# Thirteen instead of twelve seven-product blocks per MLP layer, another order of their loads, and tiles moved into the pool

## The chip, the cores and the metric

The kernel runs on one core of a Trainium2 chip. The metric is the device time of one execution in microseconds. A core has several engines with an instruction queue each: TensorE (PE, matrix products), VectorE (DVE), ScalarE (ACT), GpSimd (POOL) and SyncE (SP, which here only starts transfers), and 16 DMA engines that all queues share.

## The reference

A trunk of two layers over 256 tokens of width 2048, in float32. Each layer adds a mixer and then an MLP:

```python
x = x + mixer(rms_norm(x, norm_mix[l]))
h = rms_norm(x, norm_ffn[l])
u = jnp.einsum('bsd,df->bsf', h, w_up[l])             # 2048 -> 8192
x = x + jnp.einsum('bsf,fd->bsd', jnp.square(jax.nn.relu(u)), w_down[l])   # 8192 -> 2048
```

Layer 0's mixer is a sliding-window attention beside a state-space scan, layer 1's a dilated attention. The change lies in the MLPs' second product, the down projection; what it does in the mixers is to hold a few tiles elsewhere.

## The kernel before

**Three-product matmuls.** Every weight comes from HBM as float32 and is split into a rounded part `whi` and a rest `wlo`; the activations likewise. A product is three matmuls: hi*hi, hi*lo, lo*hi. Weights come in pieces of 256 rows by 512 columns (512 KB, two k-tiles). A plain piece works on both halves of the tokens: 2 k-tiles x 2 halves x 3 = 12 matmuls of 128x512.

**The MLP.** An up unit is 512 hidden columns: 8 pieces, 16 units per layer. Its squared ReLU is transposed into `uf` and split into `uh` and `ul`. Two up units make a chunk of 1024 hidden columns, c = 0 to 7. The down projection takes, for each chunk, four column stripes of 512, four pieces each.

**Seven.** For a chunk c and a pair of stripes, the down product can be seen as 2x2 blocks (two token halves; two halves of the chunk; two stripes), which the class `Seven` does with seven block products instead of eight. With its two halves h of each product it is 14 pieces of 6 matmuls, 84 in all, where the same work in plain units is 8 pieces of 12, 96 in all. The weight blocks are called 11, 21, 12, 22 (first digit the half of the chunk, second the stripe), each with two halves (a, b below). A seven loads 8 of them on SP's queue (`sraw`, line 262). Block sums are made in place: GpSimd starts a transfer that adds the neighbouring stripe's block to 11 and to 12 in SBUF (accumulating DMA, line 276; written 11' and 12' below), and DVE adds twice two tiles (t2 = 11' + 22, and 21 += t2). The products come in the order of the tuple SEVEN: P1 (11), P2 (21), Q6 (t2), Q7 (12'), Q5 (11'), Q4 (21'), Q3 (22). On the side of the activations P1, P2 and Q4 use halves of u, the other four use sums s1 and s2 that `operands(c)` makes. P1 is the only one that uses the first u tile of the chunk, and only its first 128 tokens. Before, 12 of the 14 pairs of chunks 0 to 6 in a layer are sevens: both pairs in chunks 0, 1, 3, 4 and 5, one in chunks 2 and 6. Chunk 7 is plain.

**The order of work.** `mlp` writes a plan, a list of pieces, which `mixed` interleaves: after the first 16 up pieces, each chunk gets n up pieces from the tuple (20, 20, 8, 20, 20, 24, 0), and the sevens' pieces are put between them from 4.5 up pieces on. So each chunk starts with five pure up pieces, then comes the first seven's first piece (P1, half a). The plan is carried out by `run`, piece by piece. At piece i it issues, in this order: `low(i+2)` (DVE: wlo = raw - whi; for a seven's P1 and P2 the accumulating transfer is issued right behind it, since it changes a raw tile whose parts have just been taken), `fetch(i+6)` (SP: the transfer of the raw tile; for a seven at P1 it fetches 11, at P2 it fetches 21, 12 and 22), `high(i+3)` (ACT: whi), `add(i+4)` (DVE sums), evictions, and the matmuls. Up pieces' raw tiles turn in a ring of RAW = 4 buffers (`wraw`, line 306), so an up piece's transfer waits on SP's queue until DVE has made the `wlo` of the up piece four before, and what stands behind it on SP's queue waits with it. The sevens' raw tiles come from the common pool `work`, tag `w4`, of 29 tiles of 4 KB per partition. The engines' side work (transposes, splits, sums, norms) is put between by `tick`, which keeps a budget per piece. All engines run their instructions in the order of emission; line 71 is the helper through which DVE, ACT and PE instructions pass.

Of the kernel before, what the change touches and what calls it, by code (L numbers as in the profile page):

```python
# [7 lines left out]
F32 = mybir.dt.float32  # L8
# [32 lines left out]
def trunk(ctx: ExitStack, tc: tile.TileContext, x, norm_mix, norm_ffn, w_up, w_down, ab_w_in, ab_q_norm,  # L41
# [193 lines left out]
    def unit(*a, **k):  # L235
# [1 line left out]

    SEVEN = (("P1", "a", "11"), ("P2", "b", "21"), ("Q6", "a", "t2"), ("Q7", "c", "12"), ("Q5", "a", "11"),  # L240
             ("Q4", "c", "21"), ("Q3", "a", "22"))
    LOADS = {"P1": ("11",), "P2": ("21", "12", "22")}
    SUMS = {"Q6": ("t2", "11", "22"), "Q4": ("21", "21", "t2")}

    class Seven:


        def __init__(self, w, rows, c0, kts, operands, to, needs, mark):
            self.w, self.rows, self.c0, self.operands, self.to, self.needs, self.mark = \
                w, rows, c0, operands, to, needs, mark  # L250
# [8 lines left out]
        def fetch(self, p, h):  # L259
            for b in LOADS.get(SEVEN[p][0], ()):  # L260
                r, c = self.rows[int(b[0]) - 1] + h * KC, self.c0 + (int(b[1]) - 1) * W
                nc.sync.dma_start(self.tile(b, h),
                                  self.w[r * 128:(r + KC) * 128, c:c + W].rearrange("(k p) c -> p k c", p=128))

        def add(self, p, h):
            if SEVEN[p][0] in SUMS:
# [1 line left out]
                x, y = self.raw[x, h], self.raw[y, h]  # L268
                V.tensor_tensor(self.raw[o, h] if o != "t2" else self.tile(o, h), x, y, op=OP.add)

        def accumulate(self, p, h):

            o = {"P1": ("11", 0), "P2": ("12", 1)}.get(SEVEN[p][0])
            if o is not None:
                r, c = self.rows[o[1]] + h * KC, self.c0 + W
                nc.gpsimd.dma_start(self.raw[o[0], h],  # L276
                                    self.w[r * 128:(r + KC) * 128, c:c + W].rearrange("(k p) c -> p k c", p=128),
                                    accum_op=OP.add)

        def source(self, p, h):  # L280
            return self.raw[SEVEN[p][2], h]
# [1 line left out]
        def evict(self, p):  # L283

            name, b, _ = SEVEN[p]
            t, j, op = {"P1": (0, 0, OP.add), "P2": (0, 0, OP.add), "Q6": (1, 0, OP.add), "Q7": (1, 1, OP.subtract),
                        "Q5": (1, 1, OP.subtract), "Q4": (1, 0, OP.add), "Q3": (0, 1, OP.subtract)}[name]
            r = self.to[t][j]
            V.tensor_tensor(r, r, self.bank[b], op=op)

    def run():
        todo = plan
# [31 lines left out]
        def low(i):  # L324
            if i < len(todo):
                raw = raws.pop(i)
                lo = wpool.tile([128, KC, raw.shape[2]], F32R, name="wlo", bufs=AHEAD + 1)
                V.tensor_tensor(lo, raw, f32(parts[i][0]), op=OP.subtract)
                parts[i].append(lo)
                u, c = todo[i]  # L330
                if isinstance(u, Seven):
                    u.accumulate(*c)

        for i in range(RAW):
            if i % 2 == 0:
# [8 lines left out]
                load_x(2 + i // 2)  # L344
            fetch(RAW + i)
        high(AHEAD)
        nc.sync.dma_start(cst[:, C_TRI:], shapes[:, C_TRI:])
        pending = []
        before = ps = None
        kept, held = [], []  # L350
        for i, (u, c) in enumerate(todo):
# [9 lines left out]
            if isinstance(u, Seven):  # L361
                p, h = c
                name, b, _ = SEVEN[p]
                if p in u.needs and h == 0:
                    need(u.needs[p])
                new = b not in u.bank
                if new:
                    u.bank[b] = aux("sp")
                sp = u.bank[b]
                xh, xl, t0 = u.operands(name)  # L370
# [250 lines left out]
                last(t, j)  # L621
        free(ps)

    def residual_unit(w, ktiles, j, needs={}, nm=None, last=None, check=None, mark=None):
        def after(ps):
            if check is not None:
                check()
# [323 lines left out]
    def mlp(layer, nm, nxt, last=None):  # L951
# [22 lines left out]
        def operands(c):  # L974

            for k in marks[c - 1] if 0 < c < NC - 2 else [("up", layer)] if c else []:
                yield from until(k)
            if c == NC - 1:
                yield from until(("uf", layer, 2 * c + 1))
            for i in (2 * c, 2 * c + 1):  # L980
                yield from until(("uf", layer, i))
                u[i] = slot("uh"), slot("ul")
                split(u[i][0], u[i][1], uf[i])
                done.add(("u", layer, i))
                yield 2
            if c == NC - 1:
                return
            a1, a2 = uf[2 * c], uf[2 * c + 1]
            s1, s2 = w4([128, 4, T], "s1"), w4([128, 4, T], "s2")
            o, n = slice(0, 128), slice(128, T)  # L990
            V.tensor_tensor(s1[:, :, o], a2[:, :, n], a1[:, :, n], op=OP.subtract)
            V.scalar_tensor_tensor(s1[:, :, n], a1[:, :, o], -1.0, s1[:, :, o], op0=OP.mult, op1=OP.subtract)
            V.tensor_tensor(s2[:, :, o], a1[:, :, o], a1[:, :, n], op=OP.subtract)
            V.scalar_tensor_tensor(s2[:, :, n], a2[:, :, o], -1.0, s1[:, :, n], op0=OP.mult, op1=OP.subtract)
            yield 2
            sums[c] = [(slot("sh"), slot("sl")) for _ in range(2)]
            for (h, l), s in zip(sums[c], (s1, s2)):
                split(h, l, s)
                yield 1
# [12 lines left out]
        def down(c, j):  # L1012
# [6 lines left out]
            def whole():  # L1019
                assert all(("down", layer, k, j) in done or ("down", layer, k, j - j % 2) in done for k in range(NC - 1))  # L1020

            return residual_unit(wd, kts, j, {4 * b: ("u", layer, 2 * c + b) for b in range(2)}, nxt, last, whole).pieces

        def seven(c, j):
            def parts(name):
                i, k, t = {"P1": (0, 0, 0), "P2": (0, 1, 0), "Q4": (0, 1, 128), "Q5": (1, 0, 0), "Q6": (1, 0, 128),
                           "Q7": (1, 1, 0), "Q3": (1, 1, 128)}[name]
                return (sums[c][k] if i else u[2 * c + k]) + (t,)

            marks[c].append(("down", layer, c, j))  # L1030
            return Seven(wd, (8 * c, 8 * c + 4), j * W, 4, parts,
                         [[res[:, t, (j + i) * W:(j + i + 1) * W] for i in range(2)] for t in range(2)],
                         {0: ("u", layer, 2 * c), 1: ("u", layer, 2 * c + 1), 2: ("sums", layer, c)},
                         marks[c][-1]).pieces

        def mixed(rest, s, start, end):

# [20 lines left out]

    n2 = Norm(R_MIX + 16, False)
    mlp(0, n1, n2)  # L1060
# [2 lines left out]
    wqkv = c_w_qkv[0]  # L1063
    oh, ol = [None] * 4, [None] * 4

    def dilated(g):
# [105 lines left out]
```

## Time and profile before

| | |
|---|---|
| time, median of 3 | 2264.33 us (2263.88 to 2264.35) |
| profiled execution, its own time | 2264.74 us |
| its span, first to last instruction | 2262.9 us |
| granted TensorE clock, mean | 1.000 |
| DMA moved | 475.10 MB, 210 GB/s in the mean |
| SP-issued `sraw` loads | 192 of 512 KB, median 8.1 us to landing |
| POOL-issued accumulating `sraw` transfers | 96 of 512 KB, median 10.7 us to landing |
| `wraw` loads of w_up | 256 of 512 KB, median 5.2 us to landing |

The profile records one execution: when each instruction ran on its engine, what released it, and when each transfer landed. Groups of instructions are written as out<-in with the program's tile names; a time to landing is counted from the issue on the queue. Matmuls overlap: one is shown as 389 ns while the next starts before it ends, so the time per matmul is read from a long row of them.

### The profile page before, as it was taken

The page shows a single profiled execution, that of the slowest core. Times are in us where ns is not written, and L with a number is a line of the kernel's source. Part 1 is how long each engine was busy: PE and PEld are TensorE (multiplying, and loading weights), DVE is VectorE, ACT ScalarE, POOL GpSimd, SP SyncE. Part 2 cuts the span into 40 slices and gives each one's busy share as a digit, 9 for nine tenths or more (in the row PEclk, how much of TensorE's full clock was granted, in tenths as well). Part 3 has the DMA queues.
Part 4 walks back from the last instruction along what each step waited for, and adds up shares of the span by engine and source line. Part 5 has one row for each costly group of instructions (what it writes and reads, how often), then busy time and mean ns, then how long its engine had stood idle before and what let it go on. Part 6 is the DMA issues. An engine that isn't in the chain of part 4 may idle for free.

```text
span 2262.9 us, 30235 instructions
## 1 busy us (share of the span) xinstructions
PE 2247.2 (99%) x11029; PEld 1873.0 (83%) x11029; DVE 1749.7 (77%) x2482; ACT 1290.0 (57%) x1615; POOL 125.7 (6%) x116
## 2 busy tenths in 40 slices
PE   8999999999999999999999999999999999999999
PEld 7998988888888888888788778778888888888877
DVE  6779986556888888887976766665588888888786
ACT  6565545445666556565664555555566665656663
POOL 1000000000001010000000000000000000010000
PEclk9999999999999999999999999999999999999999
DMA  7546555568797797888756455546788789797874
GB/s 235 163 142 190 177 177 182 190 186 246 216 296 214 209 288 222 242 245 234 219 171 192 149 158 168 168 151 186 245 237 240 206 242 281 207 282 228 248 222 141
DMA packets 255318, 475.10 MB, mean 210 GB/s; under 512 B 17156, under 2 KB 27696, under 8 KB 255168
## 3 DMA queue, kind: packets, MB, share of 16 engines
q1 hardware_dynamic: 218976, 416.34, 56.7%
q0 software_dynamic: 26624, 50.48, 12.5%
q10 hardware_dynamic: 9568, 6.34, 0.9%
q8 instruction: 86, 1.41, 0.2%
q14 instruction: 64, 0.52, 0.1%
HBM read 470.97 MB, written 2.13 MB: 209 GB/s over the span
## 4 chain that ended last, share of the span: by engine, by line
PE 97%; DMA 1%; DVE 1%; issue 1%; ACT 0%; SPq 0%; DVEq 0%; POOLq 0%; ACTq 0%
PE acc L71 71%; PE sp L71 20%; PE uT L71 1%; PE sc L71 1%; PE o L71 1%; DMA sraw<-in_w_down_dram 1%; PE pT L71 1%; PE yp L71 1%; PE xT L71 1%; DVE wlo L71 1%; DMA wraw<-in_ab_w_in_dram 0%; PE qp L71 0%; DMA res<-in_x_dram 0%; PE yo L71 0%; PE kp L71 0%
## 5 line engine op out<-in xcount | busy, mean ns | idle before, releaser
L71 ACT ACTIVATE whi<-wraw 128x1024 fp32r<-128x1024 f32 (+1 forms) x600 | 631.9, 1054 | 493.6 <-PE acc L71 350.8
L71 DVE TENSOR_TENSOR wlo<-wraw,whi 128x1024 fp32r<-128x1024 f32 (+1 forms) x600 | 725.0, 1214 | 233.7 <-PE acc L71 159.7
L71 PE MATMUL acc<-whi,hThi 128*128 128x512 f32 (+1 forms) x1632 | 647.7, 397 | 1.8 <-ACT hThi L71 1.7
L71 PE MATMUL acc<-whi,hTlo 128*128 128x512 f32 (+1 forms) x1632 | 634.8, 389 | 1.0 <-DVE hTlo L71 1.0
L71 PE MATMUL acc<-wlo,hThi 128*128 128x512 f32 (+1 forms) x1632 | 634.1, 389 | 0.7 <-DVE wlo L71 0.7
L71 ACT ACTIVATE whi<-sraw 128x1024 fp32r<-128x1024 f32 x336 | 353.7, 1059 | 292.4 <-DVE sraw L71 137.0
L71 DVE TENSOR_TENSOR wlo<-sraw,whi 128x1024 fp32r<-128x1024 f32 x336 | 408.8, 1221 | 85.3 <-PE acc L71 35.3
L71 PEld LDWEIGHTS acc<-whi,hThi 128*128 128x128 f32 x1632 | 307.6, 188 | 66.8 <-issue 5.8
L71 PEld LDWEIGHTS acc<-whi,hTlo 128*128 128x128 f32 x1632 | 307.2, 188 | 65.7 <-DVE hTlo L71 1.8
L71 PEld LDWEIGHTS acc<-wlo,hThi 128*128 128x128 f32 x1632 | 307.9, 189 | 60.9 <-DVE wlo L71 1.1
L276 POOL DMA_DIRECT2D sraw<-in_w_down_dram x96 | 117.3, 1576 | 2058.7 <-DVE wlo L71 1815.6
L71 PE MATMUL sp<-wlo,sh 128*128 128x512 f32 x384 | 149.5, 389 | 0.0
L71 PE MATMUL sp<-whi,sl 128*128 128x512 f32 x384 | 149.5, 389 | 0.0
L71 PE MATMUL sp<-whi,sh 128*128 128x512 f32 x384 | 149.4, 389 | 0.0
L71 DVE TENSOR_TENSOR sraw<-sraw 128x1024 f32<-128x1024 f32 x96 | 117.1, 1219 | 26.4 <-DMA sraw<-in_w_down_dram 26.3
L71 DVE TENSOR_TENSOR res<-res,sp 128x512 f32<-128x512 f32 x168 | 114.7, 682 | 17.4 <-PE sp L71 17.1
L71 PE MATMUL acc<-hThi,whi 128*128 128x256 f32 x384 | 112.3, 293 | 0.0
L71 PE MATMUL sp<-whi,ul 128*128 128x512 f32 x288 | 112.1, 389 | 0.0
L71 PE MATMUL sp<-whi,uh 128*128 128x512 f32 x288 | 112.0, 389 | 0.0
L71 PE MATMUL sp<-wlo,uh 128*128 128x512 f32 x288 | 112.0, 389 | 0.0
L71 PE MATMUL acc<-hThi,wlo 128*128 128x256 f32 x384 | 108.5, 283 | 0.0
L71 PE MATMUL acc<-hTlo,whi 128*128 128x256 f32 x384 | 108.5, 283 | 0.0
(221 smaller groups left out, 2749.8 us busy)
## 6 DMA issues: line engine op xcount, KB each, us to landing
wraw<-in_w_up_dram SPq DMA_DIRECT2D x256, 512.0 KB, 5.2
sraw<-in_w_down_dram SPq DMA_DIRECT2D x192, 512.0 KB, 8.1
wraw<-in_ab_w_in_dram SPq DMA_DIRECT2D x96, 512.0 KB, 3.7
sraw<-in_w_down_dram POOLq DMA_DIRECT2D x96, 512.0 KB, 10.7
wraw<-in_c_w_qkv_dram SPq DMA_DIRECT2D x96, 512.0 KB, 4.2
wraw<-in_w_down_dram SPq DMA_DIRECT2D x64, 512.0 KB, 4.2
wraw<-in_ab_w_out_dram SPq DMA_DIRECT2D x48, 512.0 KB, 3.7
wraw<-in_c_w_o_dram SPq DMA_DIRECT2D x32, 512.0 KB, 3.6
```

Source lines behind the costliest of these rows:

```text
L71: return f(out, *a, **k)
L276: nc.gpsimd.dma_start(self.raw[o[0], h], self.w[r * 128:(r + KC) * 128, c:c + W].rearrange("(k p) c -> p k c", p=128), accum_op=OP.add)
```

## The change

Thirteen of the fourteen pairs per layer become sevens: chunk 2 now has both. The up pieces per chunk become 19, 18, 18, 19, 19, 19. The pool grows from 29 to 31 tiles; masks, the keys `k0T` and `btok` are no longer held for the whole kernel but as tiles of the pool, and the second transfer of constants is cut in two (128 KB and 192 KB where 704 KB went, the rest loaded in layer 1). Of a chunk's first u only the half that P1 reads is split and kept, hi and lo in one tile (chunks 0 to 5). In a seven, Q7 and Q6 change places; at P1 the blocks 12 and 11 are fetched, at P2 21 and 22; the accumulating transfer into 12 is issued by GpSimd at once behind the issue of 12's load, instead of behind P2's `low`; that into 11 stays behind P1's `low`. Chunk 7's u no longer waits for both its tiles.

```diff
-    work = ctx.enter_context(tc.tile_pool(name="work", bufs=29))
+    work = ctx.enter_context(tc.tile_pool(name="work", bufs=31))
...
-    cst = consts.tile([128, C_ALL], F32, name="cst")
+    cst = consts.tile([128, C_M0], F32, name="cst")
...
-    mask0 = cst[:, C_M0:C_M0 + 384]
-    mask1 = cst[:, C_M1:C_M1 + 384]
-    mult1 = cst[:, C_N1:C_N1 + 384]
+    mask0 = w4([128, 384], "mask0")
...
-    SEVEN = (("P1", "a", "11"), ("P2", "b", "21"), ("Q6", "a", "t2"), ("Q7", "c", "12"), ("Q5", "a", "11"),
+    SEVEN = (("P1", "a", "11"), ("P2", "b", "21"), ("Q7", "c", "12"), ("Q6", "a", "t2"), ("Q5", "a", "11"),
              ("Q4", "c", "21"), ("Q3", "a", "22"))
-    LOADS = {"P1": ("11",), "P2": ("21", "12", "22")}
+    LOADS = {"P1": ("12", "11"), "P2": ("21", "22")}
...
                 nc.sync.dma_start(self.tile(b, h),
                                   self.w[r * 128:(r + KC) * 128, c:c + W].rearrange("(k p) c -> p k c", p=128))
+                if b == "12":
+                    self.accumulate("12", 1, h)
...
-        def accumulate(self, p, h):
-
-            o = {"P1": ("11", 0), "P2": ("12", 1)}.get(SEVEN[p][0])
-            if o is not None:
-                r, c = self.rows[o[1]] + h * KC, self.c0 + W
-                nc.gpsimd.dma_start(self.raw[o[0], h],
-                                    self.w[r * 128:(r + KC) * 128, c:c + W].rearrange("(k p) c -> p k c", p=128),
-                                    accum_op=OP.add)
+        def accumulate(self, b, half, h):
+
+            r, c = self.rows[half] + h * KC, self.c0 + W
+            nc.gpsimd.dma_start(self.raw[b, h],
+                                self.w[r * 128:(r + KC) * 128, c:c + W].rearrange("(k p) c -> p k c", p=128),
+                                accum_op=OP.add)
...
                 u, c = todo[i]
-                if isinstance(u, Seven):
-                    u.accumulate(*c)
+                if isinstance(u, Seven) and c[0] == 0:
+                    u.accumulate("11", 0, c[1])
...
-        nc.sync.dma_start(cst[:, C_TRI:], shapes[:, C_TRI:])
+        nc.sync.dma_start(cst[:, C_TRI:], shapes[:, C_TRI:C_M0])
+        nc.sync.dma_start(mask0, shapes[:, C_M0:C_M1])
...
-                    wh, wl = xh[:, q, t0:t0 + 128], xl[:, q, t0:t0 + 128]
+                    wh, wl = xh[:, q, th:th + 128], xl[:, q, tl:tl + 128]
...
-    k0T = consts.tile([128, 2, T], F32, name="k0T")
+    kb = w4([128, 2, W], "kb")
+    k0T = kb[:, 0].rearrange("p (h t) -> p h t", h=2)
...
-    btok = consts.tile([128, 4, 128], F32, name="btok")
+    btok = kb[:, 1].rearrange("p (g n) -> p g n", g=4)
...
-            if c == NC - 1:
-                yield from until(("uf", layer, 2 * c + 1))
             for i in (2 * c, 2 * c + 1):
                 yield from until(("uf", layer, i))
-                u[i] = slot("uh"), slot("ul")
-                split(u[i][0], u[i][1], uf[i])
+                if i % 2 == 0 and c < NC - 2:
+                    u[i] = slot("uhl")
+                    split(u[i][:, :, :128], u[i][:, :, 128:], uf[i][:, :, :128])
+                else:
+                    u[i] = slot("uh"), slot("ul")
+                    split(u[i][0], u[i][1], uf[i])
...
-        for c, n in enumerate((20, 20, 8, 20, 20, 24, 0)):
+        for c, n in enumerate((19, 18, 18, 19, 19, 19, 0)):
             x, o = ups[o:o + n], o + n
             if c == NC - 2:
                 x = sum((down(c, j) for j in (0, 1)), []) + sum((down(c + 1, j) for j in range(NS)), [])
                 mixed(x, seven(c, 2), 2, 19)
-            elif n == 8:
-                mixed(x + down(c, 2) + down(c, 3), seven(c, 0), 4.5, 16)
             else:
-                mixed(x, seven(c, 0) + seven(c, 2), 4.5, n + (3 if n == 24 else 0))
+                mixed(x, seven(c, 0) + seven(c, 2), 4.5, n + (3 if c == NC - 3 else 0))
...
+            if g == 0 and i == 0:
+                masks.append(w4([128, 2, 384], "masks"))
+                nc.sync.dma_start(masks[0], shapes[:, C_M1:].rearrange("p (a k) -> p a k", a=2))
+            mask1, mult1 = masks[0][:, 0], masks[0][:, 1]
```

Of the last chunk's bookkeeping (`early`, `ready`, `sevens_end`) only the place is changed in which the next norm's sums and the stores are started.

SyncE's queue at the first seven of chunk 1 in layer 0, before. `wraw` are up pieces; `sraw_6009` is 11a, 6044 is 11b, 6066, 6068 and 6070 are 21a, 12a and 22a, 6121, 6123 and 6125 are 21b, 12b and 22b; `wraw_6021` is the up piece behind P1's first half, `wraw_6095` the one behind P2's first half:

```order
L306 DMA wraw_5991<-in_w_up_dram 128x2x512
L262 DMA sraw_6009<-in_w_down_dram 128x2x512
L306 DMA wraw_6021<-in_w_up_dram 128x2x512
L262 DMA sraw_6044<-in_w_down_dram 128x2x512
L262 DMA sraw_6066<-in_w_down_dram 128x2x512
L262 DMA sraw_6068<-in_w_down_dram 128x2x512
L262 DMA sraw_6070<-in_w_down_dram 128x2x512
L306 DMA wraw_6095<-in_w_up_dram 128x2x512
L262 DMA sraw_6121<-in_w_down_dram 128x2x512
L262 DMA sraw_6123<-in_w_down_dram 128x2x512
L262 DMA sraw_6125<-in_w_down_dram 128x2x512
L306 DMA wraw_6161<-in_w_up_dram 128x2x512
```

The same place after. `sraw_5991` is 12a, 5994 is 11a, 6006 is 12b, 6009 is 11b, then 6053 and 6055 are 21a and 22a, 6080 and 6082 are 21b and 22b:

```order
L306 DMA wraw_5967<-in_w_up_dram 128x2x512
L260 DMA sraw_5991<-in_w_down_dram 128x2x512
L260 DMA sraw_5994<-in_w_down_dram 128x2x512
L260 DMA sraw_6006<-in_w_down_dram 128x2x512
L260 DMA sraw_6009<-in_w_down_dram 128x2x512
L306 DMA wraw_6031<-in_w_up_dram 128x2x512
L260 DMA sraw_6053<-in_w_down_dram 128x2x512
L260 DMA sraw_6055<-in_w_down_dram 128x2x512
L260 DMA sraw_6080<-in_w_down_dram 128x2x512
L260 DMA sraw_6082<-in_w_down_dram 128x2x512
L306 DMA wraw_6109<-in_w_up_dram 128x2x512
L306 DMA wraw_6148<-in_w_up_dram 128x2x512
```

The loads of 12 have moved ahead of those of 11: 12a from the sixth entry of this stretch to the second, 12b from the tenth to the fourth. 21b stands ninth in both. The up piece behind P2's first half (`wraw_6095`, now `wraw_6109`) has moved from the eighth entry to the eleventh, behind all eight loads of the seven.

GpSimd's queue at the same place, before: the four accumulating transfers into 11a, 11b, 12a and 12b, then the first of the chunk's second seven:

```order
L276 DMA sraw_6009<-in_w_down_dram 128x2x512
L276 DMA sraw_6044<-in_w_down_dram 128x2x512
L276 DMA sraw_6068<-in_w_down_dram 128x2x512
L276 DMA sraw_6123<-in_w_down_dram 128x2x512
L276 DMA sraw_6386<-in_w_down_dram 128x2x512
```

After: 12a, 12b, 11a, 11b, then the second seven's first:

```order
L274 DMA sraw_5991<-in_w_down_dram 128x2x512
L274 DMA sraw_6006<-in_w_down_dram 128x2x512
L274 DMA sraw_5994<-in_w_down_dram 128x2x512
L274 DMA sraw_6009<-in_w_down_dram 128x2x512
L274 DMA sraw_6349<-in_w_down_dram 128x2x512
```

The two transfers into 12 now stand ahead of those into 11, and the first of them waits for nothing but the landing of its own load.

More of the change, by code (lines that the diff above doesn't have):

```diff
@@ L236, in unit, with __init__ @@
         plan.extend(Unit(*a, **k).pieces)
-    SEVEN = (("P1", "a", "11"), ("P2", "b", "21"), ("Q6", "a", "t2"), ("Q7", "c", "12"), ("Q5", "a", "11"),
+    SEVEN = (("P1", "a", "11"), ("P2", "b", "21"), ("Q7", "c", "12"), ("Q6", "a", "t2"), ("Q5", "a", "11"),
              ("Q4", "c", "21"), ("Q3", "a", "22"))
-    LOADS = {"P1": ("11",), "P2": ("21", "12", "22")}
+    LOADS = {"P1": ("12", "11"), "P2": ("21", "22")}
     SUMS = {"Q6": ("t2", "11", "22"), "Q4": ("21", "21", "t2")}
     class Seven:
-        def __init__(self, w, rows, c0, kts, operands, to, needs, mark):
-            self.w, self.rows, self.c0, self.operands, self.to, self.needs, self.mark = \
-                w, rows, c0, operands, to, needs, mark
+        def __init__(self, w, rows, c0, kts, operands, to, needs, mark, after=None):
+            self.w, self.rows, self.c0, self.operands, self.to, self.needs, self.mark, self.after = \
+                w, rows, c0, operands, to, needs, mark, after
             self.halves = kts // KC
@@ L289, in evict @@
             V.tensor_tensor(r, r, self.bank[b], op=op)
+            if p == 6 and self.after is not None:
+                self.after()
     def run():
@@ L369, in run @@
                 sp = u.bank[b]
-                xh, xl, t0 = u.operands(name)
+                xh, xl, th, tl = u.operands(name)
                 tick(True)
@@ L622, in add_stripe, with residual_unit @@
         free(ps)
-    def residual_unit(w, ktiles, j, needs={}, nm=None, last=None, check=None, mark=None):
+    def residual_unit(w, ktiles, j, needs={}, nm=None, last=None, mark=None):
         def after(ps):
-            if check is not None:
-                check()
             add_stripe(ps, j, last)
@@ L1017, in down, with after, ready, sevens_end @@
                                      mark=marks[c][-1]).pieces
-            def whole():
-                assert all(("down", layer, k, j) in done or ("down", layer, k, j - j % 2) in done for k in range(NC - 1))
-            return residual_unit(wd, kts, j, {4 * b: ("u", layer, 2 * c + b) for b in range(2)}, nxt, last, whole).pieces
+            def after(ps):
+                if early[j]:
+                    add_stripe(ps, j, last)
+                else:
+                    add_stripe(ps, j)
+                early[j] += 1
+                ready(j, False)
+            return Unit([(wd, j * W, W)], kts, after,
+                        needs={4 * b: ("u", layer, 2 * c + b) for b in range(2)}).pieces
+        early = [1, 1, 0, 0]
+        def ready(j, stored=True):
+            if early[j] == 2:
+                if last is not None and stored:
+                    for t in range(2):
+                        last(t, j)
+                if nxt is not None:
+                    nxt.begin(j)
+        def sevens_end(j):
+            for k in (j, j + 1):
+                early[k] += 1
+                ready(k)
         def seven(c, j):
@@ L1027, in parts @@
                            "Q7": (1, 1, 0), "Q3": (1, 1, 128)}[name]
-                return (sums[c][k] if i else u[2 * c + k]) + (t,)
+                if name == "P1" and c < NC - 2:
+                    return u[2 * c], u[2 * c], 0, 128
+                return (sums[c][k] if i else u[2 * c + k]) + (t, t)
             marks[c].append(("down", layer, c, j))
@@ L1033, in seven @@
                          {0: ("u", layer, 2 * c), 1: ("u", layer, 2 * c + 1), 2: ("sums", layer, c)},
-                         marks[c][-1]).pieces
+                         marks[c][-1], (lambda: sevens_end(j)) if c == NC - 2 else None).pieces
         def mixed(rest, s, start, end):
@@ L1064, in trunk @@
     oh, ol = [None] * 4, [None] * 4
+    masks = []
     def dilated(g):
```

## Prediction

> **What bounds the kernel now.** I read the page first, then the chain of waits, then what PE waits for. The page's first part, and its fourth, the chain that ended last:
>
> ```profile
> PE 2247.2 (99%) x11029; PEld 1873.0 (83%) x11029; DVE 1749.7 (77%) x2482; ACT 1290.0 (57%) x1615; POOL 125.7 (6%) x116
> ...
> PE 97%; DMA 1%; DVE 1%; issue 1%; ACT 0%; SPq 0%; DVEq 0%; POOLq 0%; ACTq 0%
> ```
>
> PE is the chain. Its waits, by what ended them (total us, times, longest):
>
> ```profile
> PE acc L71 <- ACT uh L71: 1.5, 2, 0.7
> PE acc L71 <- DVE ul L71: 1.2, 2, 0.6
> PE acc L71 <- DVE wlo L71: 1.1, 2, 0.7
> ```
>
> The MLPs lose under 4 us to waits. So the change can gain what PE no longer computes and hardly more, but it can lose as much as it makes PE wait. A PE piece costs 6 or 12 matmuls; a long row of them in the chain gives the price of one:
>
> ```profile
> 461.45 29.95 PE acc L71 x132
> ```
>
> 29.95 / 132 = 0.2269 us. A plain piece is 2.72 us, a seven's piece 1.36 us.
>
> **The gain.** Per layer one pair of stripes goes from 96 matmuls to 84: 24 fewer in all, 24 x 0.2269 = 5.45 us off the chain. The second wait for a wlo goes too, I think. It is the one row of PE's timeline in which a seven's sum came late:
>
> ```profile
> 1902.16 0.50 PE L71 MATMUL acc<-wlo,hThi 128*128 128x512 f32 x1 [0.67 <-DVE wlo L71]
> ```
>
> The chain ahead of it runs through the accumulating transfer into 11, which t2 needed; t2 is now needed two pieces later, and the transfer starts no later. With the pipeline's refill I count 0.9 us. The waits for uh and ul belong to chunk 6, whose split isn't touched, and stay.
>
> **What DVE and ACT get.** In place of 8 plain pieces come 14, with 4 sums and 7 evictions for 4:
>
> ```profile
> L71 DVE TENSOR_TENSOR wlo<-sraw,whi 128x1024 fp32r<-128x1024 f32 x336 | 408.8, 1221 | 85.3 <-PE acc L71 35.3
> L71 DVE TENSOR_TENSOR sraw<-sraw 128x1024 f32<-128x1024 f32 x96 | 117.1, 1219 | 26.4 <-DMA sraw<-in_w_down_dram 26.3
> L71 DVE TENSOR_TENSOR res<-res,sp 128x512 f32<-128x512 f32 x168 | 114.7, 682 | 17.4 <-PE sp L71 17.1
> L71 ACT ACTIVATE whi<-sraw 128x1024 fp32r<-128x1024 f32 x336 | 353.7, 1059 | 292.4 <-DVE sraw L71 137.0
> ```
>
> DVE: 6 x 1.22 + 4 x 1.22 + 3 x 0.68 = 14.3 us more per layer; the halved splits give back 6 x about 0.6 = 3.6. A chunk of 18 up pieces and two sevens keeps PE for 18 x 2.72 + 28 x 1.36 = 87 us. DVE's work in it: 46 wlo, 8 sums, 14 evictions, and some 10 us of splits and sums of u, 56 + 10 + 10 + 10 = 86 us by these durations. It is less in truth, since neighbours on DVE overlap by about 5 hundredths (two `sl` of 1.22 us took 2.35 in the timeline):
>
> ```profile
> 636.99 2.35 DVE L71 TENSOR_TENSOR sl<-s,sh 128x1024 fp32r<-128x1024 f32 x2
> ```
>
> So DVE just keeps up, and I take nothing for it; were it bound, 2 us in each of four such chunks, 8 us, would be its price. ACT has room. The masks' later load (384 KB) and the two pool tiles lie in layer 1's mixer, where a load lands in 4.2 us in the median:
>
> ```profile
> wraw<-in_c_w_qkv_dram SPq DMA_DIRECT2D x96, 512.0 KB, 4.2
> ```
>
> They are wanted far later than that: nothing, and about 1 us if that cover were gone.
>
> **The loads, where I expect the loss.** SP's and GpSimd's queues at a first seven, here that of chunk 1 in layer 0. PE starts its P1 at 641.49 (T0):
>
> ```profile
> 641.49 0.39 PE L71 MATMUL sp<-whi,uh 128*128 128x512 f32 x1
> ```
>
> ```profile
> 624.92 0.62 SPq L262 DMA_DIRECT2D sraw<-in_w_down_dram  x1
> ...
> 633.80 0.85 SPq L306 DMA_DIRECT2D wraw<-in_w_up_dram  x1
> ```
>
> ```profile
> 637.37 1.20 POOL L276 DMA_DIRECT2D sraw<-in_w_down_dram  x1 [47.37 <-DVE wlo L71]
> 641.92 3.68 POOL L276 DMA_DIRECT2D sraw<-in_w_down_dram  x3 [3.34 <-DVE wlo L71]
> ```
>
> SP issues the first block 16.6 us ahead of T0, the accumulating transfers come 4.1 us ahead of it and later, when nearly all of the seven's loads have landed. That lead is set by SP's wait for the ring of four `wraw` buffers, which the change leaves alone:
>
> ```profile
> SPq L306 <- DVE wlo L71: 1671.1, 525, 8.4
> ```
>
> Times to landing from issue, of the transfers of four narrow windows (issued at 624.92, at 633.80, at 637.37 and at 641.92):
>
> ```profile
> sraw<-in_w_down_dram SPq DMA_DIRECT2D x1, 512.0 KB, 6.0
> ...
> wraw<-in_w_up_dram SPq DMA_DIRECT2D x1, 512.0 KB, 13.9
> ...
> sraw<-in_w_down_dram POOLq DMA_DIRECT2D x1, 512.0 KB, 9.3
> ...
> sraw<-in_w_down_dram POOLq DMA_DIRECT2D x1, 512.0 KB, 9.1
> ```
>
> And what the queues moved in the 16 us before 642, with loads alone, and in the 16 us behind, with the accumulating transfers (q0) beside the loads (q1):
>
> ```profile
> DMA packets 2922, 5.64 MB, mean 353 GB/s; under 512 B 166, under 2 KB 166, under 8 KB 2922
> ```
>
> ```profile
> q0 software_dynamic: 1048, 2.04, 68.7%
> q1 hardware_dynamic: 1142, 2.20, 40.7%
> ```
>
> Alone, a load of 0.524 MB takes 0.524 / 353 GB/s = 1.49 us. Beside accumulating transfers it takes 16 x 0.524 / 2.20 = 3.8 us, and such a transfer 16 x 0.524 / 2.04 = 4.1 us. An accumulating transfer lands 9.1 to 9.3 us after its issue and moves for 4.1 of them, so its data begins about 5 us behind the issue (an estimate).
>
> The Trainium skill has for transfers issued by GpSimd ("DMA: Bandwidth & Descriptors", section "Anatomy of one DMA — SWDGE (gpsimd) path") about 2.0 us plus the bytes at 436 GB/s, which is 3.2 us for 512 KB, 1.2 of it moving; by that the sum below would hold no stall and come to 2258. The trace disagrees, with 9.1 us and 4.1.
>
> Now the new order. SP issues 12a first, at T0 - 17; it lands 6.0 later, at -11, and GpSimd, which waits for nothing else, issues its accumulating transfer at once. The data begins at S = -6, six us earlier than before; 12b and the two into 11 follow, and the four last 4 x 4.1 = 16.4 us, to +10.4. Before, the seven's loads were past by then; now they fall into this stretch. The fourth load lands at -11 + 3 x 1.49 = -6.5. The next two I take at 2.9 us each, since the load of 633.80 landed at 647.7 and two loads fell into the 5.7 us behind 642; the later ones at 3.8 to 4.1, say 4.0, until +10.4, then 1.49. So the loads number 5 to 10 land at -4, -1.2, +2.8, +6.8, +10.5 and +12. From a landing to the matmul lie whi, 1.06, and wlo, 1.22, less 0.23, since only the second matmul reads wlo: 2.05 us.
>
> Chunks 1 and 2 (18 up pieces): PE's order is P1a 0, P1b 1.4, an up piece 2.7, P2a 5.4, P2b 6.8, an up piece 8.5 (with a transpose between). SP's order puts 21b eighth and that up piece tenth. P2b can start at 6.8 + 2.05 = 8.85: 2.05 us late. The up piece at 12 + 2.05 = 14.05, against 8.5 + 2.05: another 3.5. Together 5.6 us.
>
> Chunks 3, 4 and 5 (19): P1a 0, up piece 1.4, P1b 4.1, P2a 5.5, up piece 6.8, P2b 9.5. Here that up piece's load is eighth, 21b ninth: 8.85 against 6.8, 2.05 late; 10.5 + 2.05 = 12.55 against 11.55, another 1.0. Together 3.1 us (with rounding).
>
> Chunk 0's first seven has more lead, 547.12 less 526.12 = 21 us, and a chunk's second seven, which follows pieces that don't turn the ring, more again; that of chunk 1 683.24 less 658.99 = 24 us:
>
> ```profile
> 526.12 0.46 SPq L262 DMA_DIRECT2D sraw<-in_w_down_dram  x1
> ...
> 658.99 0.97 SPq L262 DMA_DIRECT2D sraw<-in_w_down_dram  x2
> ```
>
> ```profile
> 547.12 0.39 PE L71 MATMUL sp<-whi,uh 128*128 128x512 f32 x1
> ...
> 683.24 0.39 PE L71 MATMUL sp<-whi,uh 128*128 128x512 f32 x1
> ```
>
> With 4 us more, the load at 6.8 lands at 2.8, early enough; I count none there. The queue behind the late block on ACT and DVE holds only pieces that PE needs later still, so one lateness isn't counted again.
>
> Sum: 2 layers x (2 x 5.6 + 3 x 3.1) = 41.0 us. Against the profiled execution: 2264.74 - 5.45 - 0.9 + 41.0 = 2299.4; the median of the runs lies 0.4 below it: **2299 us**.
>
> Bounds of the stall. At 4.0 us from the first load behind S on, 21b or the up piece lands at -6.5 + 16 = 9.5, 4.75 late; with what follows 6.6 and 4.75 per chunk, 2 x (13.2 + 14.25) = 55: 2313. If the accumulating transfers cost no more of the engines than loads do, 1.49 each and half the share, they end at +6, loads eight and ten land at +5 and +8.5: 0.3 and some 1.8 us in chunks 1 and 2, little in the others, 8 us in all: 2266. My value lies by the upper end, as the 16 us that show both kinds side by side are the same sort of stretch.
>
> **The rivals.** *Hidden after all (faster).* The slices of the loads' window reach 410 GB/s, 1.28 us per transfer:
>
> ```profile
> GB/s 200 215 328 394 333 317 276 266 271 297 307 312 353 399 348 338 307 323 353 410 410 410 410 410 379 333 343 389 379 333 379 405 410 405 404 405 410 394 384 374
> ```
>
> If both kinds ran so, ten loads and four transfers would be through at -6.5 + 10 x 1.28 = 6.3, in time for 8.5. The same follows if GpSimd's descriptors take so long that the transfers into 12 begin after T0, as those into 11 do now. Then only the matmuls count: 2264.3 - 6.3 = 2258, and down to 2257 if a wait for a chunk 6 load goes too:
>
> ```profile
> 2203.40 0.50 PE L71 MATMUL acc<-wlo,uh 128*128 128x512 f32 x1 [0.42 <-DVE wlo L71]
> ```
>
> For it speaks that PE waits little now although the same twelve transfers meet at each of these places; against it the 3.8 us per load. 0.25.
>
> *A small loss (same).* Accumulating transfers at the lower price above, 2266, or a stall in chunks 1 and 2 alone of under 2.6 us each. 0.10.
>
> *DVE becomes the bound in the dense chunks.* 86 of 87 us; 8 us for four chunks, and no stall at the loads: 2266 again, or on top of the forecast 2307. It lies within the range; 0.05, counted with slower.
>
> *The forecast, stalls at the first sevens.* 0.60; its own range is 2270 (data two us later, stalls of 12 us in all) to 2313.
>
> The change could fail to do what it says only if SP were held ahead of 12; the ring's wait is the same for 11 before, so I give that nothing of its own.
>
> **How the numbers follow.** A measurement can tell about 0.2%, 4.5 us, from no change: faster is below 2259.8, slower above 2268.9. Faster 0.25, same 0.10, slower 0.65. Leaving out no more than 2 in 10 needs the fast case: 2257 to 2313.
>
> **What would show it.** In the profile after: PE waits for `wlo` or `whi` at T0 + 7 to + 14 in the first sevens of chunks 1 to 5, 5 to 6 us each in chunks 1 and 2, about 3 in the rest; SP loads of 21b and of the up piece behind P2a that take 14 to 18 us to land; GpSimd's first issue some 10 us ahead of T0 instead of 4; 2184 matmuls into `sp` where 2016 stand now; under 2 us of waits in second sevens. It is wrong if PE's waits stay under 6 us in all, or if they stand at the sums or evictions instead of the loads, or if GpSimd's transfers move at more than 200 GB/s.

## The result and the profile after

The changed kernel takes 2343.39 us in the median (2341.36 to 2346.71), the kernel before 2264.34; the ratio is 1.035 (95% interval 1.0333 to 1.0368), 79 us slower. The profiled execution took 2346.71 us, 82.0 more than that of before. The direction was forecast, the size (2299, at most 2313) was not.

The page's first part and its chain, after:

```profile
PE 2275.7 (97%) x11005; PEld 1878.8 (80%) x11005; DVE 1771.5 (76%) x2508; ACT 1296.5 (55%) x1627; POOL 133.7 (6%) x124
...
PE 81%; DMA 13%; DVE 4%; ACT 2%; issue 1%; SPq 0%; ACTq 0%; DVEq 0%
```

PE runs 24 matmuls fewer, as the change says, and DMA now carries 13% of the chain. What PE waits for, after (us, times, longest):

```profile
PE sp L71 <- DVE res L71: 23.9, 14, 3.0
PE acc L71 <- ACT whi L71: 8.5, 5, 2.8
PE acc L71 <- DVE wlo L71: 7.8, 13, 0.8
PE sp L71 <- DVE wlo L71: 5.9, 8, 0.8
PE uT L71 <- ACT relu L71: 4.9, 2, 4.1
...
PE sp L71 <- ACT whi L71: 2.2, 2, 1.9
```

The five rows of whi, wlo and relu, 29.3 us, I take for the late loads; e1 below keeps them without the largest row. That row is another matter: PE waits for DVE to add a seven's bank to `res`. The prediction had no such wait.

**The late loads** came where they were forecast. Here is PE's timeline at chunk 1 in layer 0, where T0 = 645.04:

```profile
645.04 0.39 PE L71 MATMUL sp<-whi,uhl 128*128 128x512 f32 x1
...
651.62 0.39 PE L71 MATMUL sp<-whi,ul 128*128 128x512 f32 x1
653.95 0.50 PE L71 MATMUL sp<-whi,uh 128*128 128x512 f32 x1 [1.95 <-ACT whi L71]
655.21 0.80 PE L71 MATMUL sp<-wlo,uh 128*128 128x512 f32 x1 [0.76 <-DVE wlo L71]
655.80 0.63 PE L71 MATMUL sp<-whi,ul 128*128 128x512 f32 x1
656.23 0.63 PE L71 MATMUL sp<-whi,uh 128*128 128x512 f32 x1
...
664.09 0.63 PE L71 MATMUL acc<-wlo,hThi 128*128 128x512 f32 x1
664.52 0.52 PE L71 MATMUL acc<-whi,hTlo 128*128 128x512 f32 x1
664.88 0.40 PE L71 MATMUL sp<-whi,sh 128*128 128x512 f32 x1
665.11 0.39 PE L71 MATMUL sp<-wlo,sh 128*128 128x512 f32 x1
```

P2b starts at T0 + 8.9 instead of 6.8; the forecast said 8.85. Of its transfers, four in narrow windows (issued by SP at 630.39, 630.90 and 631.92, and by GpSimd at 633.68):

```profile
wraw<-in_w_up_dram SPq DMA_DIRECT2D x1, 512.0 KB, 10.3
...
sraw<-in_w_down_dram SPq DMA_DIRECT2D x1, 512.0 KB, 13.8
...
sraw<-in_w_down_dram SPq DMA_DIRECT2D x1, 512.0 KB, 20.8
...
sraw<-in_w_down_dram POOLq DMA_DIRECT2D x1, 512.0 KB, 9.4
```

They are the loads number 5, 6 and 8 (21b) of the prediction, and the accumulating transfer into 12a. The three loads land at T0 - 4.3, -0.3 and +7.7; the forecast had -4, -1.2 and +6.8. The two behind them land at +10.4 and +11.7, forecast +10.5 and +12. GpSimd issues 11.4 us ahead of T0, against 4.1 before.

**The clock** is new. From 655.8 to 664.5 the matmuls start 0.43 us apart, not 0.227. Windows of two us show it; the third number from the right is the granted clock, and behind it stand the DMA share and GB/s:

```profile
652.00:654.00 2.00, 0.06 (x2) 0.05 (x1) 0.07 (x1) 1.06 (x1) 0.00 (x0) 1.00 1.10 257
654.00:656.00 2.00, 1.24 (x3) 0.83 (x4) 1.76 (x2) 0.00 (x0) 0.00 (x0) 0.64 1.05 380
656.00:658.00 2.00, 1.71 (x5) 0.80 (x3) 0.05 (x1) 1.14 (x2) 0.00 (x0) 0.50 1.06 407
...
662.00:664.00 2.00, 2.00 (x6) 1.61 (x5) 2.00 (x3) 0.76 (x2) 0.00 (x0) 0.50 0.10 39
664.00:666.00 2.00, 2.00 (x8) 1.59 (x7) 2.00 (x3) 0.70 (x1) 0.00 (x0) 0.80 0.00 0
```

After the wait TensorE is granted half its clock for some ten us, which costs some 4 us of the matmuls' time. The trace has ten such stretches between the first MLP and the end of the second: this one of 10.2 us, one of 6.8 and eight of 3.4, 44 us in all, of which half is lost. That agrees with the mean clock over the span, 0.990 where it was 1.000: 0.010 x 2344.9 = 23 us. The last two rows show also that the DMA engines stand idle (39 and 0 GB/s) right after the jam: it is a burst, not a lack of bandwidth over the chunk.

**The eviction.** In SEVEN's new order Q6 and Q5 stand side by side, and both add up in bank "a". Q5 may not write the bank before DVE has read it for Q6. PE at chunk 3, and DVE's queue there:

```profile
864.29 0.39 PE L71 MATMUL sp<-whi,sl 128*128 128x512 f32 x1
867.66 0.47 PE L71 MATMUL sp<-whi,sh 128*128 128x512 f32 x1 [2.98 <-DVE res L71]
867.97 0.39 PE L71 MATMUL sp<-wlo,sh 128*128 128x512 f32 x1
868.20 0.39 PE L71 MATMUL sp<-whi,sl 128*128 128x512 f32 x1
```

```profile
863.43 1.22 DVE L71 TENSOR_TENSOR wlo<-wraw,whi 128x1024 fp32r<-128x1024 f32 x1
864.56 1.22 DVE L71 TENSOR_TENSOR sraw<-sraw 128x1024 f32<-128x1024 f32 x1
865.70 1.22 DVE L71 TENSOR_TENSOR wlo<-sraw,whi 128x1024 fp32r<-128x1024 f32 x1
866.83 0.68 DVE L71 TENSOR_TENSOR res<-res,sp 128x512 f32<-128x512 f32 x1
```

Q6 ends at 864.7; its eviction stands behind a sum and a wlo and runs at 866.83. Before, Q7 (bank "c") stood between Q6 and Q5, and no such row was in PE's waits. Twelve of the 14 waits are of this kind, six of 2.65 to 2.98 us in first sevens and six of 0.87 in second ones. Ahead of the other two (0.2 and 1.2 us, chunk 5) an up piece stands between the two products.

The profiled difference closes: waits 53.2 less the 1.1 for wlo before, 52.1; clock 23; 44 waits with some 0.25 of refill each, 11 (an estimate from one place, 867.66: 3.14 lost for 2.98 waited, and 0.1 at the next matmul); matmuls -5.4; together 81 of 82.0.

### The profile page after: what moved, and what is told of

Same layout as the page of the kernel before. It is cut to its first block, busy times and chain, and to the rows that moved or that the text cites. A ratio compares the mean times of both kernels' runs of the same rounds, so it can differ in the third digit from the quotient of the medians.

```text
span 2344.9 us, 30293 instructions
## 1 busy us (share of the span) xinstructions
PE 2275.7 (97%) x11005; PEld 1878.8 (80%) x11005; DVE 1771.5 (76%) x2508; ACT 1296.5 (55%) x1627; POOL 133.7 (6%) x124
## 4 chain that ended last, share of the span: by engine, by line
PE 81%; DMA 13%; DVE 4%; ACT 2%; issue 1%; SPq 0%; ACTq 0%; DVEq 0%
PE acc L71 58%; PE sp L71 17%; DMA wraw<-in_w_up_dram 11%; DVE wlo L71 2%; ACT whi L71 1%; PE uT L71 1%; PE sc L71 1%; PE o L71 1%; PE pT L71 1%; DVE sraw L71 1%; DVE res L71 1%; PE yp L71 1%; PE xT L71 1%; DMA sraw<-in_w_down_dram 1%; DMA wraw<-in_ab_w_in_dram 0%
## 5 line engine op out<-in xcount | busy, mean ns | idle before, releaser
L71 DVE TENSOR_TENSOR wlo<-wraw,whi 128x1024 fp32r<-128x1024 f32 (+1 forms) x584 | 706.6, 1215 | 268.9 <-PE acc L71 158.3
L71 ACT ACTIVATE whi<-wraw 128x1024 fp32r<-128x1024 f32 (+1 forms) x584 | 614.6, 1054 | 505.2 <-PE acc L71 295.3
L71 ACT ACTIVATE whi<-sraw 128x1024 fp32r<-128x1024 f32 x364 | 383.6, 1059 | 351.8 <-DVE sraw L71 131.4
L71 DVE TENSOR_TENSOR wlo<-sraw,whi 128x1024 fp32r<-128x1024 f32 x364 | 443.7, 1222 | 131.2 <-ACT whi L71 50.6
L71 PE MATMUL sp<-whi,sh 128*128 128x512 f32 x416 | 164.0, 394 | 23.9 <-DVE res L71 23.9
L71 PE MATMUL sp<-wlo,sh 128*128 128x512 f32 x416 | 163.8, 394 | 0.3
L71 PE MATMUL sp<-whi,sl 128*128 128x512 f32 x416 | 163.8, 394 | 0.0
L71 PEld LDWEIGHTS sp<-whi,sh 128*128 128x128 f32 x416 | 78.8, 189 | 45.5 <-ACT whi L71 24.7
L71 PEld LDWEIGHTS sp<-wlo,sh 128*128 128x128 f32 x416 | 78.6, 189 | 18.0 <-DVE wlo L71 2.2
L71 PEld LDWEIGHTS sp<-whi,sl 128*128 128x128 f32 x416 | 78.8, 189 | 16.4
```

Of the source, the lines that this page charges most:

```text
L71: return f(out, *a, **k)
```

## The experiments

All keep the thirteen pairs, the larger pool and the half u, unless the text says otherwise. They are called e1 to e11.

**e1: Old order of products alone.**

```diff
-    SEVEN = (("P1", "a", "11"), ("P2", "b", "21"), ("Q7", "c", "12"), ("Q6", "a", "t2"), ...
+    SEVEN = (("P1", "a", "11"), ("P2", "b", "21"), ("Q6", "a", "t2"), ("Q7", "c", "12"), ...
```

> The changed kernel with the old order of products (Q6 ahead of Q7), its new loads kept. Theory: the 23.9 us in which PE waits for an eviction (14 waits, all between Q6 and Q5, which now share a PSUM bank without a product between) come from the order of products alone; they go, with their refill and some of the half-speed clock: 2305 to 2318 us, and the row of PE waiting for res is gone. Rival: these waits are only the trail of the late loads, since DVE lags behind them; then the time stays within 10 us of 2343 and other waits of DVE take their place.

Measured: 2310.42 us, ratio 1.0202 (1.0184 to 1.0221). No wait for res is left in PE's rows, of which the largest now are:

```profile
PE acc L71 <- DVE wlo L71: 7.9, 13, 0.8
PE acc L71 <- ACT whi L71: 6.7, 4, 2.8
PE sp L71 <- DVE wlo L71: 6.3, 9, 0.8
PE uT L71 <- ACT relu L71: 5.6, 5, 3.2
```

The order of products costs 33 us here, and the late loads stay without it.

**e2: Old loads and accumulating transfers, new order of products.**

```diff
-    LOADS = {"P1": ("12", "11"), "P2": ("21", "22")}
+    LOADS = {"P1": ("11",), "P2": ("21", "12", "22")}
...
-                if b == "12":
-                    self.accumulate("12", 1, h)
...
-                if isinstance(u, Seven) and c[0] == 0:
-                    u.accumulate("11", 0, c[1])
+                if isinstance(u, Seven) and c[0] < 2:
+                    u.accumulate(("11", "12")[c[0]], c[0], c[1])
```

> The changed kernel with the old fetch order and the old place of the accumulating transfers into 12 (behind P2's low), the new order of products kept. Theory: the late loads at the first sevens go with their waits for whi, wlo and relu (some 27 us) and most of the half-speed clock; the waits between Q6 and Q5 stay: 2280 to 2300 us. Rival (the eviction waits trail the late loads): 2258 to 2264 us, no row of PE waiting for res.

Measured: 2436.56 us, ratio 1.0762 (1.0745 to 1.0779), far outside both. PE's first rows:

```profile
PE sp L71 <- ACT whi L71: 45.9, 28, 4.3
PE sp L71 <- DVE res L71: 37.5, 20, 3.0
PE sp L71 <- DVE wlo L71: 24.9, 33, 1.7
```

Q7 now follows P2 at once, and the transfer into the 12 that it reads is issued only behind P2: PE waits for its whi 28 times, in nearly every seven. I had not thought of it. So, with these loads, the new order of products can't do without the early transfer into 12; what that transfer costs is read from e1, e3 and e4, which have the old order.

**e3: Both undone: thirteen pairs, pool and half u alone** (the two edits above together).

> Both undone: thirteen sevens, the larger pool and the half u, with the old products, loads and accumulating transfers. Theory: only the matmuls' gain is left, 2256 to 2260 us, clock 1.000. Rival (the denser chunks make DVE the bound, or crowd the loads by themselves): 2264 us or more.

Measured: 2265.04 us, ratio 1.0004 (0.9994 to 1.0014). The gain of 5.4 is not there. The rival had the number; which of its two reasons holds (DVE, or crowded transfers) was left to the later runs.

**e4: Late transfers into 12 alone**, with the new fetch order and old products:

```diff
-                if b == "12":
-                    self.accumulate("12", 1, h)
...
-                if isinstance(u, Seven) and c[0] == 0:
-                    u.accumulate("11", 0, c[1])
+                if isinstance(u, Seven) and c[0] < 2:
+                    u.accumulate(("11", "12")[c[0]], c[0], c[1])
```

> Old products, the new fetch order (12 and 11 at P1, 21 and 22 at P2), but the accumulating transfers into 12 issued behind P2's low as before. It tells the early accumulating transfers from the order of the loads. Theory (the early transfers take half the engines from the loads): 2256 to 2262 us. Rival (the up piece and 21b come too late because four sraw loads stand ahead of them on SP's queue): 2275 us or more, with waits for whi at the first sevens.

Measured: 2264.50 us, ratio 1.0001 (0.9991 to 1.0011). Against e1, which differs by nothing but when GpSimd issues two of four transfers, 2310.42 - 2264.50 = 45.9 us. In e1 the transfers into 11 also stand behind those into 12 on GpSimd's queue, but that isn't what costs: DVE waits 23.0 us for blocks to add there, and 51.2 here. The order of the loads on SP's queue costs nothing by itself (e3 has the old one, 2265.04). Like e3 it lies above what was expected, by 2.5 us.

**e5: Four pieces more lead**, with old products, loads and transfers:

```diff
-                fetch(i + AHEAD - 1 + RAW)
+                for j in (i + AHEAD - 1 + RAW, i + AHEAD - 1 + RAW + 4):
+                    if j < len(todo) and isinstance(todo[j][0], Seven) == (j > i + AHEAD - 1 + RAW):
+                        fetch(j)
```

> Thirteen sevens with the old products, loads and accumulating transfers (as e3_pairs_only), but the sevens' loads are fetched four pieces earlier (i+10 instead of i+6). In e3 the matmuls' 5.45 us were gone again; its waits at 658, 747 and 1836 come behind an accumulating transfer or a load that lands late. Theory (transfers land too late in the denser chunks): with four pieces more lead they land in time, 2257 to 2261 us. Rival (DVE is the bound in the chunks of 18 up pieces): no change, 2263 to 2267 us.

Measured: 2257.85 us, ratio 0.9972 (0.9961 to 0.9984), faster than both kernels. So the thirteenth pair's gain was lost to transfers that land late, not to DVE, which has the same work here. DVE's waits for a block that it is to add, in e3 and in this kernel:

```profile
DVE sraw L71 <- DMA sraw<-in_w_down_dram: 56.7, 31, 3.3
```

```profile
DVE sraw L71 <- DMA sraw<-in_w_down_dram: 38.5, 27, 3.1
```

What is left of them no longer reaches PE. The two kernels run the same matmuls in the same order. Set side by side, e3 is 7.4 us behind at the end of the profiled executions, and some 7 of them are lost in chunks 1 to 4 of the two layers. PE's rows of waits for whi and wlo in e3 hold only 2.4 us of that; the rest are smaller gaps between matmuls, which those rows leave out.

**e6: Early transfers into 12 with the old fetch order** (old products; LOADS as before, the rest as in the change).

> Thirteen sevens, old products, old fetch order, but the accumulating transfers into 12 are issued at the fetch of 12's load. The load of 12a now stands fourth among the sevens' loads and not first, so its accumulating transfer begins some 5 us later than in the changed kernel. Theory (what hurts is accumulating data ahead of the loads, not the early issue as such): 2258 to 2268 us. Rival (any issue that doesn't wait for P2 hurts): 2280 us or more.

Measured: 2370.06 us, ratio 1.0467 (1.0453 to 1.0482). The rival's number, but not by late loads: its waits are at the sums. DVE at the first seven of chunk 1:

```profile
652.69 1.22 DVE L71 TENSOR_TENSOR sraw<-sraw 128x1024 f32<-128x1024 f32 x1 [5.88 <-DMA sraw<-in_w_down_dram]
...
660.24 1.23 DVE L71 TENSOR_TENSOR sraw<-sraw 128x1024 f32<-128x1024 f32 x1 [4.60 <-DMA sraw<-in_w_down_dram]
```

On GpSimd's queue each transfer into 11 now stands behind one into 12: the four land at 648.65 (12a), 652.66 (11a), 656.50 (12b) and 660.22 (11b), so 11' comes 8.5 and 16.0 us behind the seven's first matmul at 644.19. The sum t2, which Q6 needs first, waits for 11', and behind the sum on DVE stands the wlo of the next up piece.

**e7: Early transfers, four pieces more lead, old products** (the edits of e1 and e5).

> As e1_old_products (new fetch order, early accumulating transfers into 12, old products), with the sevens' loads four pieces earlier. e1 took 2310 us. Theory (the transfers take the engines from loads that PE needs 7 to 9 us behind T0; they all shift by some 10 us): the loads land in time, 2257 to 2263 us. Rival (the transfers slow the loads whenever they run, so the stall only moves to other loads): 2280 us or more.

Measured: 2260.62 us, ratio 0.9985 (0.9976 to 0.9994). The same loads and transfers cost 50 us less than in e1. At chunk 1 the first block is issued 32.7 us ahead of T0 where it was 16.9, and 21b lands 4.9 us ahead of T0 where it landed 7.8 behind. Against e5, which has the late transfers into 12, it is 2.8 us slower.

**e8: The changed kernel with the lead alone.**

> The changed kernel whole (new order of products too), with the sevens' loads four pieces earlier. With late loads out of the way it shows the order of products by itself. Theory (Q6 and Q5 share a PSUM bank without a product between, PE waits for the eviction in more than half of the 26 sevens, 1.7 us and 0.3 of refill each, and some half-speed clock): e7 plus 25 to 38 us, PE waiting for res over 20 us. Rival (the eviction is late only where late loads have put DVE behind): within 8 us of e7.

Measured: 2277.33 us, ratio 1.0057 (1.0043 to 1.007), 16.7 above e7; less than the 25 expected at least, more than the rival's 8. PE's first row:

```profile
PE sp L71 <- DVE res L71: 13.4, 12, 2.4
```

In the plan of thirteen pairs Q6's second half stands right before Q5's first in 12 of the 26 sevens (all those of chunks 0, 3 and 4, by `mixed`'s own arithmetic), and these are the 12 waits. With loads in time ten of them are short, 1.03 us from one matmul to the next beyond the usual, and two are 2.5. So both were partly right: the adjacency makes the wait, and late loads, which put DVE behind, make it about twice as dear (33 us).

**e9: Twelve pairs, the kernel before, with the lead.**

> The kernel before with only the sevens' loads four pieces earlier. It tells whether the lead is a gain by itself or only makes room for the thirteenth pair. Theory (with twelve pairs the transfers are late in one place, worth 0.9 us, and the matmuls are as many as before): 2262.5 to 2264.5 us. Rival (the lead alone gives the 6 us of e5): 2257 to 2260 us.

Measured: 2263.20 us, ratio 0.9994 (0.9985 to 1.0003). The lead makes room for the thirteenth pair and does little else.

**e10: Two pieces of lead instead of four** (old products, loads and transfers).

> As e5_lead4 with two pieces more lead instead of four (i+8). Theory: lateness in e3 was 0.7 to 1.7 us at the PE, two up pieces are 5.4 us, so two are enough: 2257 to 2259 us. Rival (the transfers only get through with the whole lead): between e3's 2265 and e5's 2258, 2260 to 2264 us.

Measured: 2262.19 us, ratio 0.9989 (0.998 to 0.9998). The rival's case: two pieces are not enough. PE still waits for a wlo at chunk 2:

```profile
PE sp L71 <- DVE wlo L71: 0.6, 1, 0.6
```

That row is small. Of the 4.4 us between the two profiled executions, 1.7 lie at the very start, where this one has a stretch at half the clock (19.5 to 22.9 us) that e5's hasn't. The other 2.7 are lost in the MLPs, 2.5 of them at chunks 1 and 2 of layer 0, again mostly in gaps too small for the rows of waits. So two pieces of lead bring back more than half of the 7 us that e3 loses there.

**e11: Q6's eviction first on DVE**, in the changed kernel with the lead: it is kept in a list `urgent`, which is emptied ahead of `low`.

```diff
-                    pending.append(lambda u=u, p=p: u.evict(p))
+                    (urgent if name == "Q6" else pending).append(lambda u=u, p=p: u.evict(p))
```

> As e8_lead4_after (2277 us), with Q6's eviction issued ahead of the next piece's low and of the sums on DVE, not behind them. In e8 PE waited 12 times between Q6 and Q5, as often as the plan has no up piece between the two, ten times for about a us and twice for 2.5. Theory (the wait is PE's for the bank, its floor the eviction itself): the two long ones shrink, the ten stay: 2271 to 2276 us, still 12 waits for res. Rival (the wait is only the eviction's place behind other work on DVE): the row is gone, 2262 us or less.

Measured: 2280.34 us, ratio 1.007 (1.0055 to 1.0085).

```profile
PE sp L71 <- DVE res L71: 11.2, 12, 1.2
PE acc L71 <- DVE ul L71: 3.5, 2, 1.7
```

The waits behave as the theory says, 12 of them and none over 1.2; the time is 3 us worse than e8, not better, and the row for ul has grown from 1.5 us to 3.5. By the profiled executions, which lie 5.6 us apart, 5.1 are lost at the two waits for ul in chunk 6: each is 1.0 us longer, and behind each comes a stretch of 3.4 us at half the clock, which e8 hasn't. DVE now stands still for PE ahead of its evictions, 61.3 us in all where it was 28.8. That this makes ul late is my reading and not shown.

## Why the prediction was wrong

*The gain of 5.45 and 0.9 us*: the count of matmuls was right. e5 is 6.3 us under the kernel before by its ratio of 0.9972, and e9, with the lead and without the thirteenth pair, some 1 us, so about 5 us are the pair's. The 0.9 us came by luck: e9 has lost its waits for wlo through the lead, not because t2 is needed later, and in the changed kernel these waits rose from 1.1 to 13.7 us. The step "DVE just keeps up, and I take nothing for it" looked at the wrong resource. With before's own loads the denser chunks lose the gain to late transfers (e3, e4), which the prediction charged to the early accumulating transfers alone. 2264.50 - 2257.85 = 6.6 us.

*The stall at the first sevens, 41.0 us*: the landings were forecast within a us, and the cost, 45.9 us between e1 and e4, lies 5 above the sum. It holds two errors that offset each other in part. Direct waits of PE are less than forecast: in e1 the four rows above and 3.5 us of another whi row make 30. The half-speed clock and the refill behind these waits, which the stall's sum didn't have, add the rest: a mean clock of 0.994 is 14 us of e1's span, and 34 waits at 0.25 are some 8. That makes 52, against 52.6 between e1 and e5, which has no such waits. There is a slip in the sum as well: at 2.9 us each the fifth and sixth load land at -3.6 and -0.7, not -4 and -1.2, and with those behind them the stall comes to some 43 instead of 41.

*What was left out altogether, the failed step that weighs most*: the exchange of Q6 and Q7 was read for when a sum is needed ("t2 is now needed two pieces later"), and the evictions were counted as DVE's work ("4 sums and 7 evictions for 4"). PE's wait for the bank that Q6 and Q5 share was put at nothing, without a reason. It is 33 us beside the late loads (e1) and 16.7 without them (e8 and e7). The order of the plan and the second entry of each product in SEVEN show the shared bank without a chip.

Together 2299 + 6.6 + 4.9 + 33.0 = 2343.5, against 2343.39. The sum closes by construction, since e5, e4, e1 and the change follow one another by an edit or two; undone in another order they would have other prices, as 16.7 for 33 shows.

*The signs* came in part. GpSimd's lead and the place of the waits behind T0 were as forecast, and 21b and the up piece took 20.8 and 22.0 us to land instead of 14 to 18. The second sevens, which were to have under 2 us of waits, have 5.2 us for evictions alone. One of the signs of being wrong came too: the largest row stands at the evictions.

*The rivals*: "hidden after all" falls by the traces; the Trainium skill's figure for GpSimd's transfers ("DMA: Bandwidth & Descriptors", "Anatomy of one DMA — SWDGE (gpsimd) path"), on which it could have rested, is again not what the trace shows, 9.4 us against its 3.2. "DVE becomes the bound" falls by e5. "A small loss" falls by the 45.9 us of the early transfers. The change without its new order of products and without these transfers does measure 2265.04 and 2264.50 (e3, e4), no difference that can be told from before, but there the lost gain is the reason.

## What to carry to other kernels

Where an engine has hardly waited, the profile doesn't show what a wait costs beyond itself: on TensorE here ten stretches at half the clock, of 3.4 to 10.2 us, followed upon waits and cost some 22 us. When the order of accumulating products is changed, look for neighbours that share a PSUM bank and are read between. And a transfer that is issued earlier is paid for by those that it overtakes (e1, e6): shift the whole group rather than one of its members (four pieces of lead for all of a seven's loads, 2257.85 us with the old transfers and 2260.62 with the early ones).

## What was not expected of the hardware

The granted clock fell to 0.50 at chunk 1 in the second of two waits of PE, of 1.95 and 0.76 us, and behind a single wait of 2.96 us in chunk 0, but not behind one of 2.98 us in chunk 3 (867.66, the matmuls behind it 0.23 to 0.31 apart):

```profile
572.28 0.47 PE L71 MATMUL sp<-whi,sh 128*128 128x512 f32 x1 [2.96 <-DVE res L71]
```

```profile
569.20:572.60 3.40, 0.44 (x3) 0.31 (x3) 3.40 (x5) 2.00 (x2) 0.00 (x0) 1.00 1.08 257
572.60:576.00 3.40, 3.40 (x12) 2.72 (x11) 3.03 (x3) 0.24 (x1) 1.19 (x1) 0.50 1.05 407
...
862.80:866.10 3.30, 1.88 (x9) 1.22 (x7) 3.30 (x4) 0.77 (x2) 0.00 (x0) 1.00 0.95 257
866.20:869.50 3.30, 1.84 (x8) 1.59 (x9) 3.30 (x4) 2.85 (x4) 1.07 (x1) 1.00 1.09 266
```

The trace offers a reason. The ten stretches at 0.50 begin at 572.62, 654.54, 756.94, 968.57, 1050.49, 1702.44, 1787.77, 1883.34, 2077.90 and 2098.38, all whole multiples of 3.413 us apart, and last one, two or three times as long. On this grid the 2.96 us lie within one window (569.21 to 572.62), while a boundary at 866.17 halves the 2.98 us. The wait of 2.98 us at 1997.58 is divided in the same way (1995.98), and the clock stayed at 1.00 there too.

The Trainium skill ("TensorE: Matmul & The Clock Gate", section "Part 1: The HAM clock gate (the "warmup" mystery)") says that TensorE goes to half its clock when a free-running window of about 3.4 us was idle and back after a busy one. The trace agrees in the value, 0.50, and in the window's length and its running on regardless of the waits. It differs in that a window need not be idle throughout: in the one ahead of 654.54 PE started four matmuls. How much work in a window keeps the clock, no run here measures. The return took 10.2 us at chunk 1, with gaps between the matmuls at first, and 3.4 us in eight of the ten.

Accumulating transfers beside plain loads kept the rates of before: 9.4 us to landing for the first one, as against 9.3, and about 4.0 us from load to load (the sixth and eighth land at 644.7 and 652.7).
